# A two-block network on one core: which loads stand ahead of the first gathered rows, and where the last output product and two weight splits are put

## The chip, the cores and the metric

One core of a Trainium2 chip runs one program. The metric is the device time of an execution in microseconds (us); lower is better. Engines: TensorE (PE, its weight loads PEld), VectorE (DVE), ScalarE (ACT), GpSimd (POOL) and SyncE (SP). SP computes nothing: it issues most DMA transfers, one after the other, and each waits in this order for what it needs.

## The reference

Two transformer-like blocks over 512 tokens of 1024 features, in float32. The first has attention, a recurrent scan and a feed-forward net; the second has a convolution, attention, a cross attention and a mixture of experts. Only the end of the second matters here:

```python
x = x + cross_attention(rmsnorm(x, norm_xa_g[l]), rmsnorm(mem, norm_mem_g[l]), ...)   # o @ wo
x = x + hierarchical_moe(rmsnorm(x, norm_moe_g[l]), ...)
return rmsnorm(x, norm_final_g)

def hierarchical_moe(h, wg, bg, we, be, w_gate, w_up, w_down):
    ...            # router: best of 4 groups, best 2 of its 4 experts, their weights -> combine
    a = jnp.einsum("nd,edf->nef", hf, w_gate)
    b = jnp.einsum("nd,edf->nef", hf, w_up)
    u = jax.nn.silu(a) * b * combine[..., None]
    y = jnp.einsum("nef,efd->nd", u, w_down)
```

There are 16 experts with 256 inner features; each token goes to two.

## The kernel before

All float32 products are made from a high and a low part: `wsplit` (L350) writes a weight tile's high part with ACT (L354) and its low part with DVE (L357), and each k-step of `mm_as` (L375) is three matmuls (L380, L381, L382). The order of instructions on each engine is fixed when the program is built, by a list scheduler that goes by data, by buffers and by the order in which the code was written; `issue_after` keeps an instruction behind another one on its engine.

**Cross attention.** Tokens are four tiles of 128 (t = 0 to 3). `cross_out(t)` multiplies a tile by the output weights in two halves of 512 columns (n = 0, 1; 12 matmuls each) and DVE adds each half to the residual `x` (L1421). `route_unit(t)` then squares the row on ACT (L1463), transposes `x` on PE (L1467, tile `tp`), copies it (`xT`, L1470 and L1472), multiplies by the router's weights (L1481), finds group and experts on DVE (L1483 to L1511), and stores the normalised rows `hr` to DRAM (`rows_d`, L1503). When all four tiles are done, `slot_ids` (L1553) has the list of tokens of each expert, 96 at most.

**Experts.** The generator `expert(i)` (L1657) gathers its rows from `rows_d` with an indirect DMA that POOL issues (L1668, tile `gat`), transposes them (L1675), splits them (`eh`) and the four weight tiles `wl` (`ws`), multiplies 24 times, applies silu and product (`eu`), splits half of its down weights (`wed` to `wdh`, `wdl`; L1698), multiplies (the second half of the columns in plain float32, L1721) and adds its rows to DRAM. Seventeen experts run in a pipe (the 17th is a spare for an overfull expert).

**Loads.** An expert's weights are four transfers of 512 KB (`wl<-w_gu`, L347, into 20 buffers shared with other tiles) and four of 256 KB (`wed<-w_ed`, L1646): 3 MiB. The generator `fetch_all` lists them: the up weights of experts 0, 1 and 2, then by turns the down weights of expert i and the up weights of expert i + 3. PF2 of its steps are taken during the cross attention, NF = 4 (L1740) at each turn of the expert loop:

```python
for n, _ in enumerate(both()):
    if n >= PF0 and (n - PF0) % PF1 == 0 and n < PF0 + PF2 * PF1:
        next(self.fetches)
```

One step is one up transfer, or the four down transfers of an expert. PF2 = 18 steps are experts 0 to 3's up weights and experts 0 and 1's down weights; expert 4's up weights come at the first turn of the loop.

Of the kernel before, what the change touches and what calls it, by code (L numbers as in the profile page):

```python
# [14 lines left out]
AF = mybir.ActivationFunctionType  # L15
ALU = mybir.AluOpType
# [6 lines left out]
NT = 4  # L23
# [9 lines left out]
FD, NF = 2, 4  # L33
# [21 lines left out]
CAP = 96  # L55
NX = 2 * S // CAP
HEADS = (slice(0, 64), slice(64, 128))
LAG = (1, 1, 1, 1)
PF0, PF1, PF2 = 2, 1, 18


def f32(ap):
# [3 lines left out]
def fl(t):  # L66
    return t.rearrange("p a b -> p (a b)")
# [111 lines left out]
def run(gen):  # L179
    for _ in gen:  # L180
        pass


def chain(*gens):
    for g in gens:
        yield from g


def pipe(gens, width, newest=False):

    act, gens = [], iter(gens)
    while True:
        if len(act) < width:
            g = next(gens, None)
            if g is not None:
                act.append(g)
        if not act:
            return
        for g in act[::-1] if newest else list(act):
            if next(g, g) is g:  # L200
                act.remove(g)
        yield


def take(gen, n):
    for _ in range(n):
        if next(gen, gen) is gen:
            return
        yield
# [15 lines left out]
class Block:  # L225
# [18 lines left out]
    def open(self, ctx):  # L244
        self.xp = self.sb(ctx, "xp")
        self.wk = self.sb(ctx, "work")
        self.n = N1
        self.nsplit, self.stage = -1, 0
        nc, ins = self.nc, self.ins
        self.x = [self.xt("x") for _ in range(NT)]  # L250
        self.load_x(0, 2)
        nc.sync.dma_start(self.ident, ins["ident"])
        nc.sync.dma_start(self.vec, ins["vec"])
        self.w_lora = [self.load(ins["w_lora"][:, g:g + 2, :], 160) for g in range(0, KD, 2)]
        self.load_x(2, 4)
# [88 lines left out]

    def load(self, src, n=512, tag="r"):
        t = self.pt("wl", F32, tag)[:, :src.shape[1], :n]
        self.nc.sync.dma_start(t, src)  # L347
        return t

    def wsplit(self, t, tags="hl"):  # L350

        nc = self.nc
        hi, lo = (self.pt("ws", F32R, g)[:, :t.shape[1], :t.shape[2]] for g in tags)
        nc.scalar.activation(hi, t, AF.Copy)  # L354
        self.nsplit += 1
        eng = nc.gpsimd if self.nsplit % 4 in SP[self.stage] else nc.vector
        eng.tensor_tensor(lo, t, f32(hi), ALU.subtract)  # L357
        return [(hi[:, j], lo[:, j]) for j in range(t.shape[1])]
# [16 lines left out]
    def mm_as(self, ps, ws, act, t, m=128):  # L375
        nt = self.nc.tensor
        sl = slice(t * m, (t + 1) * m)
        for k, (wh, wl) in enumerate(ws):
            ah, al = act[k]
            nt.matmul(ps, ah[:, sl], wh, start=k == 0, stop=False)  # L380
            nt.matmul(ps, ah[:, sl], wl, start=False, stop=False)  # L381
            nt.matmul(ps, al[:, sl], wh, start=False, stop=k == len(ws) - 1)  # L382

    def proj(self, src, act, use, rest=None, ws=None):

# [1027 lines left out]
    def cross_out(self, t, wo, z):  # L1413
        yield
        yield
        a = [(z[:, 0, h * 128:(h + 1) * 128], z[:, 1, h * 128:(h + 1) * 128]) for h in range(4)]
        for n in range(2):
            ps = self.ps("mm")
            self.mm_as(ps, wo[n], a, 0)
            x = self.x[t][:, n]  # L1420
            self.nc.vector.tensor_tensor(x, x, ps, ALU.add)  # L1421
        yield


# [215 lines left out]
    def fetch_down(self, i):  # L1640

        w = []
        for ed in self.ed[i]:
            for k in range(2):
                w.append(self.ut("wed"))
                self.nc.sync.dma_start(w[-1], ed[:, k])  # L1646
        self.ed[i] = w
        yield

# [7 lines left out]
    def expert(self, i, add=True, skip=dict(bounds_check=S - 1, oob_is_err=False)):  # L1657

        nc = self.nc

        def lag(n):
            for _ in range(LAG[n]):
                yield

        raw = self.ew.pop(i)
        g = fl(self.xt("gat"))[:CAP]

        nc.gpsimd.indirect_dma_start(out=g, out_offset=None, in_=self.rows, **skip,  # L1668
                                     in_offset=bass.IndirectOffsetOnAxis(ap=self.ids[:CAP, i:i + 1], axis=0))
        yield from lag(3)  # L1670
        a = []
        for q in range(2):
            ps = self.ps("tp")[:, :4 * CAP]
            for k in range(4):
                nc.tensor.transpose(ps[:, k * CAP:(k + 1) * CAP], g[:, (4 * q + k) * 128:(4 * q + k + 1) * 128],  # L1675
                                    self.ident[:CAP, :CAP])
            z = self.pt("eh", F32R)
            h, l = (z[:, n, :4 * CAP] for n in range(2))
            self.split_to(h, l, ps)
            a += [(h[:, k * CAP:(k + 1) * CAP], l[:, k * CAP:(k + 1) * CAP]) for k in range(4)]  # L1680
        self.stage = 6
        with ExitStack() as c:

            for ins in self.last_of if i < 2 else ():
                c.enter_context(self.tc.issue_after(ins.ins))
            wg = [w for t in raw for w in self.wsplit(t)]
        yield from lag(0)
        ps = self.ps("mm")[:CAP]
        self.mm_as(ps, wg, a, 0, CAP)
        u = self.at("eu")[:CAP, :256]  # L1690
        nc.scalar.activation(u, ps[:, :256], AF.Silu)
        nc.vector.scalar_tensor_tensor(u, u, self.ws[:CAP, i:i + 1], ps[:, 256:], ALU.mult, ALU.mult)
        yield from lag(1)

        ed = self.ed.pop(i)
        hi, lo = self.pt("wdh", F32R, "r"), self.pt("wdl", F32R, "r")
        for k in range(2):
            self.split_to(hi[:, k], lo[:, k], ed[k])  # L1698
        wd = [(hi[:, k], lo[:, k]) for k in range(2)]
        tp = self.ps("tp")  # L1700
        for k in range(2):
            nc.tensor.transpose(tp[:, k * CAP:(k + 1) * CAP], u[:, k * 128:(k + 1) * 128], self.ident[:CAP, :CAP])
        z, zf = self.tg("euT", "a", F32R), self.at("euF")
        self.split_to(z[:, :2 * CAP], z[:, 256:256 + 2 * CAP], tp[:, :2 * CAP])
        nc.scalar.copy(zf[:, :2 * CAP], tp[:, :2 * CAP])
        a = [(z[:, k * CAP:(k + 1) * CAP], z[:, 256 + k * CAP:256 + (k + 1) * CAP]) for k in range(2)]
        yield from lag(2)
        if add:
            y = self.kt("ey")[:CAP]
        else:  # L1710
            oh = self.tg("oh", "u", F32R)[:CAP]
            self.onehot(oh, i)
            yh, yl = (self.pt("yl", F32R)[:CAP] for _ in range(2))
            self.last += [(oh, yh), (oh, yl)]
        for n in range(2):
            ps = self.ps("mm")[:CAP]
            if n == 0:
                self.mm_as(ps, wd, a, 0, CAP)
            else:
                for k in range(2):  # L1720
                    nc.tensor.matmul(ps, zf[:, k * CAP:(k + 1) * CAP], ed[2 + k], start=k == 0, stop=k == 1)  # L1721
            if not add:
                self.split_to(yh[:, n], yl[:, n], ps)
            else:
                nc.scalar.copy(y[:, n], ps)
        if add:
            nc.gpsimd.indirect_dma_start(
                out=self.acc, out_offset=bass.IndirectOffsetOnAxis(ap=self.ids[:CAP, i:i + 1], axis=0),
                in_=fl(y), in_offset=None, compute_op=ALU.add)
        yield  # L1730

    def moe(self, out):
        with ExitStack() as c:
            self.psum(c, "moe", mm=4, tp=3, r=1)
            p = pipe((self.expert(i, i < LAST) for i in range(17)), 16)
            ps, self.last = self.ps("r"), []
            self.route_weights()
            more = chain(self.weigh(self.ws[:CAP, 0:16], ps[:CAP, 0:16], self.rk, self.asg, 16), self.route_more())
            for n, _ in enumerate(p):
                run(take(self.fetches, NF))  # L1740
                for _ in range(6 if n == 0 else 2):
                    next(more, None)
                if n == GB:
                    gb = self.bcast_row(3)
            xs = [self.xt("fx") for _ in range(NT)]
            hs = [self.pt("fh") for _ in range(NT)]
            self.final(out, gb, xs, hs, self.last)
# [100 lines left out]
```

## Time and profile before

| | |
|---|---|
| time, median of 3 runs | 1434.97 us (1433.1 to 1436.15) |
| the profiled execution | 1433.15 us, of which the span of instructions is 1431.3 us |
| busy share of the span | PE 95%, PEld 75%, DVE 61%, ACT 44%, POOL 4% |
| chain that ended last, by engine | PE 84%, DVE 9%, DMA 2%, ACT 2% |

The span lies 1.85 us below the execution's own time. A busy PE includes matmuls that wait in its pipeline. The cross attention ends near 1213 us, the routing near 1227, the experts run from 1236 to about 1411, and the final norm ends the span at 1431.3.

### The profile page before, as it was taken

The page shows a single profiled execution, that of the slowest core. Times are in us where ns is not written, and L with a number is a line of the kernel's source. Part 1 is how long each engine was busy: PE and PEld are TensorE (multiplying, and loading weights), DVE is VectorE, ACT ScalarE, POOL GpSimd, SP SyncE. Part 2 cuts the span into 40 slices and gives each one's busy share as a digit, 9 for nine tenths or more (in the row PEclk, how much of TensorE's full clock was granted, in tenths as well). Part 3 has the DMA queues.
Part 4 walks back from the last instruction along what each step waited for, and adds up shares of the span by engine and source line. Part 5 has one row for each costly group of instructions (what it writes and reads, how often), then busy time and mean ns, then how long its engine had stood idle before and what let it go on. Part 6 is the DMA issues. An engine that isn't in the chain of part 4 may idle for free.

```text
span 1431.3 us, 21684 instructions
## 1 busy us (share of the span) xinstructions
PE 1364.3 (95%) x8366; PEld 1073.1 (75%) x8366; DVE 874.6 (61%) x2035; ACT 623.3 (44%) x1143; POOL 52.6 (4%) x45
## 2 busy tenths in 40 slices
PE   5999999999799999999999999999999999699996
PEld 5877777677588888888888887776788887466663
DVE  5247465664875235434467475996555566799875
ACT  5244335543344333322434414445432453477873
POOL 0000000000000000000000000000000000232211
PEclk9999999999999999999999999999999999699998
DMA  5222420021223223233143214222131535799984
GB/s 209 102 76 76 156 78 20 13 90 60 89 75 118 88 89 118 71 107 118 61 146 109 84 45 162 75 74 75 62 117 60 176 134 198 239 310 335 330 285 146
DMA packets 67759, 178.01 MB, mean 124 GB/s; under 512 B 17144, under 2 KB 18552, under 8 KB 67648
## 3 DMA queue, kind: packets, MB, share of 16 engines
q1 hardware_dynamic: 58676, 156.39, 32.7%
q0 software_dynamic: 3584, 10.10, 3.2%
q10 hardware_dynamic: 5388, 10.06, 2.0%
q8 instruction: 68, 1.11, 0.3%
q14 instruction: 43, 0.35, 0.1%
HBM read 163.12 MB, written 15.88 MB: 125 GB/s over the span
## 4 chain that ended last, share of the span: by engine, by line
PE 84%; DVE 9%; DMA 2%; ACT 2%; issue 2%; SPq 0%; DVEq 0%; ACTq 0%
PE mm L371 11%; PE mm L372 11%; PE mm L373 11%; PE mm L380 10%; PE mm L382 10%; PE mm L381 10%; PE q L967 3%; PE mm L1721 2%; DVE ws L357 2%; PE acc L537 2%; PE s L512 1%; PE tp L531 1%; DVE cacc L1113 1%; PE mm L918 1%; PE tp L918 1%
## 5 line engine op out<-in xcount | busy, mean ns | idle before, releaser
L357 DVE TENSOR_TENSOR ws<-wl,ws 128x1024 fp32r<-128x1024 f32 (+2 forms) x238 | 280.6, 1192 | 140.4 <-ACT ws L354 134.0
L354 ACT ACTIVATE ws<-wl 128x1024 fp32r<-128x1024 f32 (+2 forms) x238 | 244.2, 1033 | 182.4 <-PE mm L382 111.0
L371 PE MATMUL mm<-hT,ws 128*128 128x512 f32 (+3 forms) x872 | 314.5, 365 | 1.6 <-ACT qT L565 0.7
L372 PE MATMUL mm<-hT,ws 128*128 128x512 f32 (+3 forms) x872 | 314.1, 362 | 1.0 <-DVE hT L427 1.0
L373 PE MATMUL mm<-hT,ws 128*128 128x512 f32 (+3 forms) x872 | 312.6, 361 | 0.0
L371 PEld LDWEIGHTS mm<-hT,ws 128*128 128x128 f32 (+2 forms) x872 | 162.0, 187 | 30.6 <-ACT qT L565 1.4
L372 PEld LDWEIGHTS mm<-hT,ws 128*128 128x128 f32 (+2 forms) x872 | 163.0, 187 | 27.2 <-DVE hT L427 2.4
L373 PEld LDWEIGHTS mm<-hT,ws 128*128 128x128 f32 (+2 forms) x872 | 162.8, 187 | 24.9 <-DVE ws L357 0.2
L380 PE MATMUL mm<-ws,ff 128*128 128x512 f32 x256 | 100.0, 391 | 0.0
L382 PE MATMUL mm<-ws,ff 128*128 128x512 f32 x256 | 99.7, 389 | 0.0
L381 PE MATMUL mm<-ws,ff 128*128 128x512 f32 x256 | 99.6, 389 | 0.0
L1113 DVE SCALAR_TENSOR_TENSOR cacc<-sig,vec,cacc 128x507 f32<-128x507 f32 (+25 forms) x120 | 86.1, 732 | 1.6
L1068 DVE TENSOR_TENSOR ur<-ur 128x512 f32<-128x512 f32 x32 | 22.1, 692 | 82.3 <-ACT ff L1067 82.3
L380 PE MATMUL mm<-ws,eh 128*96 128x512 f32 x136 | 56.3, 414 | 1.6 <-ACT eh L423 1.6
L1064 ACT ACTIVATE ur<-mm 128x512 f32<-128x512 f32 x32 | 19.0, 594 | 87.1 <-PE mm L373 87.1
L382 PE MATMUL mm<-ws,eh 128*96 128x512 f32 x136 | 55.7, 410 | 0.7 <-DVE eh L424 0.6
L382 PEld LDWEIGHTS mm<-ws,ff 128*128 128x128 f32 x256 | 48.0, 188 | 10.0
L381 PEld LDWEIGHTS mm<-ws,ff 128*128 128x128 f32 x256 | 48.1, 188 | 9.9
L380 PEld LDWEIGHTS mm<-ws,ff 128*128 128x128 f32 x256 | 48.1, 188 | 9.9
L381 PE MATMUL mm<-ws,eh 128*96 128x512 f32 x136 | 55.0, 404 | 0.0
L521 ACT ACTIVATE sp<-sp,mx 128x128 f32<-128x128 f32 (+3 forms) x64 | 35.7, 558 | 29.8 <-DVE mx L519 29.1
L1087 DVE TENSOR_TENSOR f<-f,mm 128x512 f32<-128x512 f32 x24 | 16.5, 686 | 49.8 <-PE mm L382 49.8
(436 smaller groups left out, 2351.0 us busy)
## 6 DMA issues: line engine op xcount, KB each, us to landing
wl<-w_gu SPq DMA_DIRECT2D x68, 512.0 KB
wl<-w_p SPq DMA_DIRECT2D x60, 512.0 KB
wed<-w_ed SPq DMA_DIRECT2D x68, 256.0 KB
wl<-w_up SPq DMA_DIRECT2D x32, 512.0 KB
wl<-w_dn SPq DMA_DIRECT2D x32, 512.0 KB
wl<-w_out SPq DMA_DIRECT2D x16, 512.0 KB
x<-x SPq DMA_DIRECT2D x8, 512.0 KB
gram_d<-gb SPq DMA_DIRECT2D x8, 256.0 KB
```

The lines of the kernel that those rows point to most:

```text
L354: nc.scalar.activation(hi, t, AF.Copy)
L357: eng.tensor_tensor(lo, t, f32(hi), ALU.subtract)
L371: nt.matmul(ps, wh[:, c0:c0 + m], ah[:, sl], start=k == 0, stop=False)
L372: nt.matmul(ps, wh[:, c0:c0 + m], al[:, sl], start=False, stop=False)
L373: nt.matmul(ps, wl[:, c0:c0 + m], ah[:, sl], start=False, stop=k == len(ws) - 1)
L380: nt.matmul(ps, ah[:, sl], wh, start=k == 0, stop=False)
L381: nt.matmul(ps, ah[:, sl], wl, start=False, stop=False)
L382: nt.matmul(ps, al[:, sl], wh, start=False, stop=k == len(ws) - 1)
L521: nc.scalar.activation(sps[h][:, :n], sps[h][:, :n], AF.Exp, scale=-1.0, bias=mxs[h][:, 0:1], accum_out=ls[h])
L537: nc.tensor.matmul(out_ps[64 * h:64 * h + 64, i * 128:(i + 1) * 128], vs[h](j), pts[h][:, j * 128:(j + 1) * 128], start=j == 0, stop=j == i)
L967: nc.tensor.matmul(ps[a], lhs[a], rhs[a], start=n == 0, stop=n == len(terms) - 1)
L1113: nc.vector.scalar_tensor_tensor(acc[:, d:], up[:, 0:S - d], w(30 - d), acc[:, d:], ALU.mult, ALU.add)
```

## The change

```diff
-PF0, PF1, PF2 = 2, 1, 18
+PF0, PF1, PF2 = 2, 1, 13
...
     def load(self, src, n=512, tag="r"):
         t = self.pt("wl", F32, tag)[:, :src.shape[1], :n]
-        self.nc.sync.dma_start(t, src)
+        self.hold(self.nc.sync.dma_start(t, src))
         return t
+
+    def hold(self, dma):
+
+        if self.behind is not None:
+            self.tc.add_manual_dep(dma.ins, self.behind.ins.name, ...)
...
             self.nc.vector.tensor_tensor(x, x, ps, ALU.add)
+            if n == 0 and t == NT - 1:
+                yield
...
-        nc.gpsimd.indirect_dma_start(out=g, out_offset=None, in_=self.rows, **skip,
+        ga = nc.gpsimd.indirect_dma_start(out=g, out_offset=None, in_=self.rows, **skip,
...
+        if i == 0:
+            self.behind = ga
...
+            wg = [w for t in raw[:2] for w in self.wsplit(t)] if i == 0 else []
             for ins in self.last_of if i < 2 else ():
                 c.enter_context(self.tc.issue_after(ins.ins))
-            wg = [w for t in raw for w in self.wsplit(t)]
+            wg += [w for t in raw[len(wg) // 2:] for w in self.wsplit(t)]
...
-        for k in range(2):
-            self.split_to(hi[:, k], lo[:, k], ed[k])
+        with ExitStack() as c:
+
+            if i < 2:
+                c.enter_context(self.tc.issue_after(act.ins))
+                c.enter_context(self.tc.issue_after(mul.ins))
+            for k in range(2):
+                self.split_to(hi[:, k], lo[:, k], ed[k])
...
             for n, _ in enumerate(p):
-                run(take(self.fetches, NF))
-                for _ in range(6 if n == 0 else 2):
+                run(take(self.fetches, NF + (5 if n == 0 else 0)))
+                self.behind = None
+                for _ in range(2 if n > 1 else 0):
                     next(more, None)
```

In the cross attention only 13 steps of loads are taken: the up weights of experts 0 to 2 and the down weights of expert 0. The other five, with expert 4's four, come at the first turn of the expert loop, and each of these is made to wait for the first gather to have landed (`hold`). `cross_out(3)` hands on between its halves. Two weight tiles of expert 0 may be split before the routing's end, and the splits of experts 0's and 1's down weights stand behind their silu and product. The weighing (`weigh`, L1543) is written behind the first expert's product, the planning of the spare (`route_more`) starts two turns later, and the second expert's transposes stand behind that product.

On SP, where the loads of the last stage begin, before (`wl<-w_gu` is an up transfer, `wed<-w_ed` a down transfer, `rows_d<-hr` the store of a token tile's rows):

```order
L347 DMA wl<-w_gu 128x1024 x12
L1503 DMA rows_d<-hr 128x1024
L347 DMA wl<-w_gu 128x1024
L1646 DMA wed<-w_ed 128x512 x4
L347 DMA wl<-w_gu 128x1024 x3
L1503 DMA rows_d<-hr 128x1024
L1646 DMA wed<-w_ed 128x512 x4
L1503 DMA rows_d<-hr 128x1024
L347 DMA wl<-w_gu 128x1024
L1503 DMA rows_d<-hr 128x1024
L347 DMA wl<-w_gu 128x1024 x3
L1646 DMA wed<-w_ed 128x512 x4
```

and in the change, from the third of the four row stores on, with the semaphores that each one waits for (`DMASW0` is that of POOL's gather):

```order
L1513 DMA rows_d<-hr 128x1024 [waits DMAHW6_49,DVE_49]
L1513 DMA rows_d<-hr 128x1024 [waits DMAHW0_49,DVE_49]
L347 DMA wl<-w_gu 128x1024 [waits DMASW0_49,DMAHW1_49,PE_49,Activation_49]
L347 DMA wl<-w_gu 128x1024 [waits DMAHW4_49,DMAHW2_49]
L347 DMA wl<-w_gu 128x1024 [waits DMAHW3_49,PE_49]
L347 DMA wl<-w_gu 128x1024 [waits PE_49,Activation_49]
L1656 DMA wed<-w_ed 128x512 [waits DMAHW5_49]
L1656 DMA wed<-w_ed 128x512 [waits DMAHW6_49]
L1656 DMA wed<-w_ed 128x512 [waits DMAHW7_49]
L1656 DMA wed<-w_ed 128x512 [waits DMAHW0_49]
L347 DMA wl<-w_gu 128x1024 [waits DMAHW1_49,Activation_49]
```

Before, eight up transfers and four down transfers stand between the first row store and the last up transfer that comes ahead of expert 2's down weights. In the change these twelve stand behind the last row store, and the first of them waits for the gather; all that follow on SP wait with it.

On PE at the end of the cross attention, before (`x_3451` is `x` of t = 2, `x_4201` that of t = 3; `mm_11021` is the second half of t = 3's output product):

```order
L380 MATMUL mm_11021<-ws_10291,oX_10792 128x512
L381 MATMUL mm_11021<-ws_10292,oX_10792 128x512
L382 MATMUL mm_11021<-ws_10291,oX_10792 128x512
L1467 MATMUL tp_11039<-ident_64,x_3451 128x128 x4
L1467 MATMUL tp_11045<-ident_64,x_3451 128x128 x4
L1481 MATMUL mm_11067<-cst_65,xT_11035 128x24 x4
L1467 MATMUL tp_11098<-ident_64,x_4201 128x128 x4
L1481 MATMUL mm_11067<-cst_65,xT_11035 128x24 x4
```

and in the change (`mm_10991` and `mm_11037` are the two halves of t = 3):

```order
L388 MATMUL mm_10991<-ws_10280,oX_10790 128x512
L389 MATMUL mm_10991<-ws_10279,oX_10790 128x512
L1477 MATMUL tp_11009<-ident_64,x_3451 128x128 x4
L1477 MATMUL tp_11015<-ident_64,x_3451 128x128 x4
L387 MATMUL mm_11037<-ws_10285,oX_10790 128x512
L388 MATMUL mm_11037<-ws_10286,oX_10790 128x512
L389 MATMUL mm_11037<-ws_10285,oX_10790 128x512
```

The eight transposes of t = 2 move from behind the second half to between the halves.

On DVE in the same place, before (`hr` is of t = 2; the `x` rows are the two adds of t = 3, and the first is not shown here):

```order
L325 SCALAR_TENSOR_TENSOR nr_q<-nr_q 128x1
L326 SCALAR_TENSOR_TENSOR nr_o<-nr_q,nr_o 128x1
L1421 TENSOR_TENSOR x<-x,mm 128x512
L1502 SCALAR_TENSOR_TENSOR hr<-x,nr_o,gbc 128x1024
L1472 COPY xT<-tp 128x512
L1483 SCALAR_TENSOR_TENSOR cst<-mm,nr_o,cst 128x24
L1485 MAX cst<-cst 128x8
L1472 COPY xT<-tp 128x512
```

and in the change:

```order
L326 SCALAR_TENSOR_TENSOR nr_o<-nr_q,nr_o 128x1
L1482 COPY xT<-tp 128x512
L1512 SCALAR_TENSOR_TENSOR hr<-x,nr_o,gbc 128x1024
L364 TENSOR_TENSOR ws<-wl,ws 128x1024
L1429 TENSOR_TENSOR x<-x,mm 128x512
L1493 SCALAR_TENSOR_TENSOR cst<-mm,nr_o,cst 128x24
L1495 MAX cst<-cst 128x8
L1496 MAX_INDEX gi<-cst 128x8
L1498 TENSOR_TENSOR og<-cst,gi 128x4
L1482 COPY xT<-tp 128x512
```

The low part of one of expert 0's weight tiles (`ws<-wl,ws`) now stands ahead of the last add to `x`, and the copy `xT` of t = 2 ahead of `hr`.

## Rows read from the trace of the kernel before

**Rows 1.** Busy time by stretch: busy us of each engine, granted clock, DMA share, GB/s

```profile
1230.00:1240.00 10.00, 3.13 (x16) 1.95 (x15) 5.52 (x12) 2.29 (x4) 6.84 (x4) 0.50 1.01 313
1240.00:1250.00 10.00, 9.30 (x39) 6.55 (x40) 5.94 (x13) 5.33 (x8) 0.96 (x1) 0.78 0.72 200
1250.00:1260.00 10.00, 9.95 (x47) 6.31 (x46) 10.00 (x61) 7.78 (x15) 1.46 (x2) 1.00 0.97 306
1260.00:1384.00 124.00, 124.00 (x590) 82.24 (x588) 106.58 (x191) 98.03 (x161) 32.61 (x23) 1.00 1.03 328
```

**Rows 2.** Moved by the DMA engines, 1230 to 1384.3 us, by queue

```profile
GB/s 356 309 237 178 218 284 303 300 335 298 284 295 336 325 304 368 322 356 321 314 343 366 311 315 300 366 349 354 318 316 348 297 356 310 316 347 265 371 406 316
DMA packets 18274, 49.04 MB, mean 318 GB/s; under 512 B 2745, under 2 KB 2745, under 8 KB 18261
q1 hardware_dynamic: 14901, 39.57, 73.3%
q0 software_dynamic: 3360, 9.31, 26.5%
```

**Rows 3.** The chain that ended last, 1350 us on: start, us, what

```profile
1374.49 9.69 DMA wl<-w_gu
...
1388.24 0.43 PE mm L382
...
1391.23 0.24 PE mm L380
```

**Rows 4.** Timeline of ACT at the end of the expert stage

```profile
1384.26 1.06 ACT L354 ACTIVATE ws<-wl 128x1024 fp32r<-128x1024 f32 x1 [3.62 <-DMA wl<-w_gu]
1385.23 0.85 ACT L423 ACTIVATE eh<-tp 128x384 fp32r<-128x384 f32 x2
```

**Rows 5.** Timeline of SP, the queue that issues the loads

```profile
1134.46 33.50 SPq L347 DMA_DIRECT2D wl<-w_gu  x12
...
1184.87 0.97 SPq L347 DMA_DIRECT2D wl<-w_gu  x1
...
1187.87 5.92 SPq L347 DMA_DIRECT2D wl<-w_gu  x3
...
1202.86 2.25 SPq L1646 DMA_DIRECT2D wed<-w_ed  x4
...
1219.22 0.33 SPq L347 DMA_DIRECT2D wl<-w_gu  x1
...
1223.95 2.90 SPq L347 DMA_DIRECT2D wl<-w_gu  x3
1227.19 1.98 SPq L1646 DMA_DIRECT2D wed<-w_ed  x4
```

**Rows 6.** Timeline, first gather to the first expert's transposes

```profile
1228.13 1.25 POOL L1668 DMA_INDIRECT gat<-rows_d,cst  x1 [458.49 <-DMA wl<-w_gu]
...
1236.27 1.54 PE L1675 MATMUL tp<-ident,gat 96*128 96x96 f32 x8 [5.22 <-DMA gat<-rows_d,cst]
```

**Rows 7.** The gathered tile over the whole run, last line of its view

```profile
DMA to landing us min/median/max: 6.0/7.6/11.0
```

**Rows 8.** Timeline of the routing of the last two token tiles

```profile
1213.20 0.69 DVE L1421 TENSOR_TENSOR x<-x,mm 128x512 f32<-128x512 f32 x1 [1.52 <-PE mm L382]
...
1220.55 0.15 DVE L331 TENSOR_SCALAR ms<-ssq 128x1 f32<-128x1 f32 x1
...
1227.00 0.16 DVE L1553 SCALAR_TENSOR_TENSOR cst<-r,ide 96x16 int32<-96x16 f32 x1
```

**Rows 9.** Timeline, split of the second expert's down weights in the cross stage

```profile
1206.66 1.30 ACT L423 ACTIVATE wdh<-wed 128x512 fp32r<-128x512 f32 x2 [4.44 <-DMA wed<-w_ed]
```

**Rows 10.** What SP waited for, 1180 to 1400 us: total, times, longest

```profile
SPq L347 <- DMA wl<-w_gu: 31.3, 23, 2.7
SPq L1646 <- DMA wed<-w_ed: 21.8, 28, 2.5
SPq L1646 <- PE mm L1721: 14.5, 5, 4.8
```

More of the change, by code (lines that the diff above doesn't have):

```diff
@@ L247, in open @@
         self.n = N1
-        self.nsplit, self.stage = -1, 0
+        self.nsplit, self.stage, self.behind = -1, 0, None
         nc, ins = self.nc, self.ins
@@ L346, in load @@
         t = self.pt("wl", F32, tag)[:, :src.shape[1], :n]
-        self.nc.sync.dma_start(t, src)
+        self.hold(self.nc.sync.dma_start(t, src))
         return t
+    def hold(self, dma):
+        if self.behind is not None:
+            self.tc.add_manual_dep(dma.ins, self.behind.ins.name,
+                                   mybir.DependencyInfo(mybir.DependencyClass.Sync, mybir.DependencyReason.DATA),
+                                   reason="hold")
     def wsplit(self, t, tags="hl"):
@@ L381, in mm_as @@
             nt.matmul(ps, ah[:, sl], wl, start=False, stop=False)
-            nt.matmul(ps, al[:, sl], wh, start=False, stop=k == len(ws) - 1)
+            o = nt.matmul(ps, al[:, sl], wh, start=False, stop=k == len(ws) - 1)
+        return o
     def proj(self, src, act, use, rest=None, ws=None):
@@ L1645, in fetch_down @@
                 w.append(self.ut("wed"))
-                self.nc.sync.dma_start(w[-1], ed[:, k])
+                self.hold(self.nc.sync.dma_start(w[-1], ed[:, k]))
         self.ed[i] = w
@@ L1673, in expert @@
             ps = self.ps("tp")[:, :4 * CAP]
-            for k in range(4):
-                nc.tensor.transpose(ps[:, k * CAP:(k + 1) * CAP], g[:, (4 * q + k) * 128:(4 * q + k + 1) * 128],
-                                    self.ident[:CAP, :CAP])
+            with ExitStack() as c:
+                if i == 1:
+                    c.enter_context(self.tc.issue_after(self.last_of[2].ins))
+                for k in range(4):
+                    nc.tensor.transpose(ps[:, k * CAP:(k + 1) * CAP], g[:, (4 * q + k) * 128:(4 * q + k + 1) * 128],
+                                        self.ident[:CAP, :CAP])
             z = self.pt("eh", F32R)
@@ L1682, in expert @@
         with ExitStack() as c:
+            wg = [w for t in raw[:2] for w in self.wsplit(t)] if i == 0 else []
             for ins in self.last_of if i < 2 else ():
                 c.enter_context(self.tc.issue_after(ins.ins))
-            wg = [w for t in raw for w in self.wsplit(t)]
+            wg += [w for t in raw[len(wg) // 2:] for w in self.wsplit(t)]
         yield from lag(0)
         ps = self.ps("mm")[:CAP]
-        self.mm_as(ps, wg, a, 0, CAP)
+        last = self.mm_as(ps, wg, a, 0, CAP)
+        if i == 0:
+            self.last_of.append(last)
+            run(self.weights)
         u = self.at("eu")[:CAP, :256]
-        nc.scalar.activation(u, ps[:, :256], AF.Silu)
-        nc.vector.scalar_tensor_tensor(u, u, self.ws[:CAP, i:i + 1], ps[:, 256:], ALU.mult, ALU.mult)
+        act = nc.scalar.activation(u, ps[:, :256], AF.Silu)
+        mul = nc.vector.scalar_tensor_tensor(u, u, self.ws[:CAP, i:i + 1], ps[:, 256:], ALU.mult, ALU.mult)
         yield from lag(1)
@@ L1696, in expert @@
         hi, lo = self.pt("wdh", F32R, "r"), self.pt("wdl", F32R, "r")
-        for k in range(2):
-            self.split_to(hi[:, k], lo[:, k], ed[k])
+        with ExitStack() as c:
+            if i < 2:
[3 more added lines that the diff above has]
+                self.split_to(hi[:, k], lo[:, k], ed[k])
         wd = [(hi[:, k], lo[:, k]) for k in range(2)]
@@ L1737, in moe @@
             self.route_weights()
-            more = chain(self.weigh(self.ws[:CAP, 0:16], ps[:CAP, 0:16], self.rk, self.asg, 16), self.route_more())
+            self.weights = self.weigh(self.ws[:CAP, 0:16], ps[:CAP, 0:16], self.rk, self.asg, 16)
+            more = self.route_more()
             for n, _ in enumerate(p):
-                run(take(self.fetches, NF))
-                for _ in range(6 if n == 0 else 2):
+                run(take(self.fetches, NF + (5 if n == 0 else 0)))
+                self.behind = None
+                for _ in range(2 if n > 1 else 0):
                     next(more, None)
```

## The prediction

> **What bounds the kernel now.** The page's chain is 84% PE, an average over a program with several stages; the change touches only the last, so I read that stage. First the stretches [rows 1]: from 1260 to 1384 us PE is busy for all 124 us, which looks like PE's bound. But the same row has the 16 DMA engines at a share of 1.03 and 328 GB/s. Both are full, and a full PE row cannot say which of the two waits, since waiting matmuls count as busy. The view by queue [rows 2] has no slice below 265 GB/s from 1250 on; over all of it went 49.04 MB in 154.3 us, 73.3% of the time for SP's loads (39.57 MB) and 26.5% for POOL's gathers and sums (9.31 MB). The chain of waits decides [rows 3]: near the end it leaves PE and goes through an up-weight load, issued at 1374.49 and taking 9.69 us. ACT stands idle 3.62 us for it and splits it at 1384.26 [rows 4]; behind that split, in ACT's fixed order, stands the split of gathered rows `eh` (1385.23) that PE needs next. SP's own waits agree [rows 10]: 31.3 and 21.8 us for earlier loads to land, against 14.5 for a matmul to free a buffer. So the experts are fed ahead at first, the lead shrinks, and at the last expert it is gone. What ends the kernel is the landing of the last expert's first load, 47.0 us before the span's end; that lands when all bytes ahead of it have moved.
>
> Ahead of the stage it is different: after the routing PE waits for the first gather. POOL issued it at 1228.13 and PE transposed its rows at 1236.27, after 5.22 us of idling [rows 6], with the clock at 0.50 of full, its 1.2 GHz level [rows 1].
>
> **The change, part by part.**
>
> *Loads.* Before, experts 3 and 4's up weights and expert 1's down weights were issued between 1184.87 and 1226.85, beside the cross attention and the routing [rows 5]; all but the tail of the last one was through by 1230. That is 8 x 512 KB and 4 x 256 KB, 5.24 MB. After the change all of it waits for the gather, and everything behind it on SP (the weights of experts 2 and 5 to 16) waits too. SP computes nothing, so only ACT's splits and PE behind them can feel it. What is the price of 5.24 MB in a full stage? SP's queue took 73.3% of 154.3 us, 113.1 us, for 39.57 MB [rows 2]: 2.86 us a MB, **+15.0 us**. The best slice (406 GB/s) gives 12.9, the stretch 1240 to 1250 (200 GB/s [rows 1]) 26.2; I take the mean of the stage, whose kind of traffic it is.
>
> *When the loads start.* The gather's issue moves by the routing (below) from 1228.13 to about 1227.1. From issue to landing the 17 gathers took 6.0 to 11.0 us, median 7.6 [rows 7]; the first took 8.1. With no load in flight I take the low end, 6.0: landed at 1233.1. Less cannot be excluded; the floor is one issue (1.25 us [rows 6]) and 0.39 MB (96 rows of 4 KB) at 328 GB/s, 1.2 us. For the first held bytes to flow I add 1.5: no row has an idle queue's first byte, the bounds are SP's 0.33 us for an issue [rows 5] and about 3 us (1202.86 to the split at 1206.66, less 0.75 us for 256 KB at 350 GB/s [rows 5, 9]). So 1234.6 instead of 1230, **+4.6**. The gather's own 0.39 MB lies ahead of that point now, **-1.2**.
>
> The Trainium skill speaks against the hold (DMA: Bandwidth & Descriptors, section Queues, rings and completion order): each DMA engine takes the queues with work by turns, packet by packet, so a gather is not behind all that SP has queued. By that it would lose no more than its own 1.2 us to the loads, and land at 1234.0 instead of 1233.1, 0.9 us more in the sum. The 6.0 us in the full stage [rows 7] fit that better than a queue behind megabytes.
>
> *What the stage can give back.* Between 1230 and 1260 the DMA engines moved 313, 200 and 306 GB/s against 328 later [rows 1]: 1.65 MB less than they could. Here the 20 buffers were full of weights loaded ahead: rows 10 have SP waiting for matmuls (longest 4.8 us). With buffers empty at the gather this hole closes: **-5.0** (0 if it was something else).
>
> *Routing.* The eight transposes of t = 2 move ahead of the second half of t = 3's product, so DVE has t = 2's copy and logits earlier. In the trace the last add to `x` is at 1213.20, t = 2's choices run on DVE up to t = 3's norm at 1220.55, and the list of tokens is at 1227.00 [rows 8]. About half a us of t = 2's work leaves DVE's row behind t = 3's copy, and expert 0's and 1's down splits no longer stand in it; against it one low split of 1.2 us stands ahead of the last add. I take 1 us gained, bounds 3 gained and 1.2 lost; it is in the 4.6.
>
> *Down splits, early up splits, weighing.* Costed at nothing. Two down splits and the 4.44 us for which ACT waited for expert 1's load [rows 9] leave the cross attention, where PE has its own matmuls in front; after the change they lie beside the second expert's 24 up matmuls. Without that cover they cost 2 x 1.3 us, once. Expert 1's down weights come behind expert 3's 2 MiB: 3.15 MB at 2.86 from 1234.6, about 1244, and one round trip. By then PE has two experts' up products and one down product in front; a stall there moves no byte and so not the end.
>
> *Sum.* 15.0 + 4.6 - 1.2 - 5.0 = **+13.4 us**, on the profiled execution's 1433.15: 1446.6. On the median, 1434.97, it would be 1448.4; I give **1447**. With halves of the bounds taken together the case's own range is 1440 to 1455.
>
> **The rivals.**
>
> *PE's bound, faster.* If the last wait of 3.62 us were an accident and the DMA engines had room, the held bytes would be absorbed and the start would count: PE begins 1236.27 - 1233.1 = 3.2 us earlier, and up to 3.6 of the wait goes. 1426 to 1430, say 1429. It decides from the point where the last expert's load lands before PE wants it. For it: the early experts have a lead of tens of us (expert 4's weights are issued by 1226.85 and its turn comes four experts later). Against it: the chain ends in a load, and the two queues' shares sum to 99.8% [rows 2]. A page of the Trainium skill gives this rival its argument: Perfetto Trace Analysis, section Identifying the Most-Contended Engine, holds that the share of busy DMA engines misleads and moved bytes should be read, and HBM Reference, section Specifications (TRN2), has about 425 GB/s for one core alone; by that figure (an estimate) 5.24 MB cost 12.3 us and the stage would have a quarter of its capacity unused. No slice of rows 2 is above 406 GB/s, and gathers of single rows share them. Chance 0.12.
>
> *Absorbed, no change.* SP's waits for buffers are starved loads, not just full ones: if all of the 14.5 us [rows 10] and not 5.0 come back, the sum is +3.9; with a gather 3 us sooner it is 1434. For it: rows 10. Against: the share of 1.03 beside those waits. 1432 to 1438, chance 0.08.
>
> *Slower still.* When the lead is gone each of the last experts waits, not only one, and PE's clock follows: after the wait at the end a matmul still takes 0.43 us at 1388.24 and 0.24 only at 1391.23 [rows 3]; the first is the lower level's pace. Some 4 us at half the pace lose 2. Three more such dips, where PE then comes later than the loads, bring 6 us: 1450 to 1458. Chance 0.12.
>
> The hold itself is certain to act: the order lists the gather's semaphore on the first held load.
>
> **How the numbers follow.** Forecast 0.68, the three rivals 0.12, 0.08, 0.12. A change below 0.2% (2.9 us) can't be told from none here. Slower: 0.68 + 0.12 = 0.80; same 0.08 (part of its cases slower, as many faster); faster 0.12. The range reaches down to the edge of the absorbed case and up through most of the slower one: 1436 to 1456, which leaves out the faster rival and a few of either end.
>
> **What would show it.** Right: SP idle from the last row store to about 1233; the first transposes some 3 us earlier; the DMA engines full from 1235 to about 1397 without the hole at 1240; ACT waiting for up weights at several of the last experts, the chain going through loads, and the last expert's first split 12 to 14 us later than 1384.26. Wrong: that split before 1388, or no waits for loads; then the stage was PE's. If the gather lands as late as before, the contention was not its delay.

## The result, and the profile after

The changed kernel takes 1445.26 us, median of 4 runs (1443.47 to 1449.17), against 1434.69 us for the kernel before (4 runs, 1433.10 to 1436.15): a ratio of 1.0069, 95% interval 1.0053 to 1.0086, or **10.6 us slower**. The forecast was 1447, slower.

The profiled execution after is the slowest of the four (1449.17 us, span 1447.4), and part of that has nothing to do with the change: it is late before the changed code begins. In the timeline of SP, the first twelve loads of experts' weights, at 1134.46 us in [rows 5], begin 5.95 us later:

```profile
1140.41 33.10 SPq L347 DMA_DIRECT2D wl<-w_gu  x12
...
1205.51 22.95 SPq L1513 DMA_DIRECT2D rows_d<-hr  x3
1238.34 1.97 SPq L347 DMA_DIRECT2D wl<-w_gu  x4
```

So 5.95 is taken off every time of after that is set beside one of before. The spans then differ by 1447.4 - 1431.3 - 5.95 = 10.15 us, close to the 10.6 us between the medians. The third row is the hold: after the last row stores SP issues nothing until 1238.34 (1232.39 when corrected).

The timelines of POOL and PE answer to [rows 6]:

```profile
1232.69 2.11 POOL L1678 DMA_INDIRECT gat<-rows_d,cst  x1 [458.67 <-DVE cst L1580]
...
1238.25 1.54 PE L1690 MATMUL tp<-ident,gat 96*128 96x96 f32 x8 [7.00 <-DMA gat<-rows_d,cst]
```

Corrected, the gather is issued at 1226.74 instead of 1228.13 and its rows are transposed at 1232.30 instead of 1236.27: 5.56 us after its issue instead of 8.14. That part of the change works: PE begins the experts 4.0 us sooner.

What it gives for that is in the stretches, counted from the first transposes (columns as in [rows 1]: PE, PEld, DVE, ACT, POOL busy, clock, DMA share, GB/s):

```profile
1238.25:1248.25 10.00, 9.46 (x43) 6.80 (x43) 5.45 (x10) 5.50 (x9) 2.20 (x3) 0.78 0.97 279
1248.25:1258.25 10.00, 7.60 (x45) 5.48 (x46) 9.81 (x23) 6.03 (x7) 0.67 (x1) 1.00 1.03 347
1258.25:1268.25 10.00, 9.78 (x40) 5.83 (x38) 9.38 (x53) 7.55 (x15) 2.48 (x2) 0.83 1.04 375
1268.25:1399.79 131.54, 123.43 (x580) 80.35 (x578) 103.03 (x195) 93.84 (x160) 31.35 (x22) 1.00 1.03 333
```

PE was busy for all 124 us of the long stretch of [rows 1]; now it is idle for 8.1 of 131.5. The DMA engines are busy from the start, without the hole that the kernel before has at 1240 us. By queue, from the first held load to the last expert's first split (1238.3 to 1399.8 us):

```profile
DMA packets 19824, 53.76 MB, mean 333 GB/s; under 512 B 2885, under 2 KB 2885, under 8 KB 19809
...
q1 hardware_dynamic: 16602, 44.74, 77.7%
q0 software_dynamic: 3207, 8.85, 24.4%
```

Against [rows 2] SP's queue has 5.17 MB more to bring behind the gather: the 5.24 MB of the forecast, but for what was under way at the edges. What waits for it shows in ACT's waits from 1230 us (total, times, longest) and in its timeline:

```profile
ACT wdh L431 <- DMA wed<-w_ed: 18.3, 11, 4.2
...
ACT ws L361 <- DMA wl<-w_gu: 6.2, 7, 3.7
```

The same view of the kernel before, from 1230 us, has nearly as much waiting for up weights and next to none for down weights:

```profile
ACT ws L354 <- DMA wl<-w_gu: 4.7, 4, 3.6
ACT wdh L423 <- DMA wed<-w_ed: 0.3, 1, 0.3
```

The timeline of ACT after:

```profile
1276.30 0.63 ACT L431 ACTIVATE wdh<-wed 128x512 fp32r<-128x512 f32 x1 [4.19 <-DMA wed<-w_ed]
...
1297.19 0.63 ACT L431 ACTIVATE wdh<-wed 128x512 fp32r<-128x512 f32 x1 [2.68 <-DMA wed<-w_ed]
...
1399.79 1.06 ACT L361 ACTIVATE ws<-wl 128x1024 fp32r<-128x1024 f32 x1 [3.73 <-DMA wl<-w_gu]
```

The last row answers to [rows 4]: 1393.84 corrected, against 1384.26, 9.6 us later. The first two rows are not at the end of the stage but near its start, and they wait for down weights. The chain that ended last says the same; it now runs through loads (start, us, what):

```profile
1284.65 12.52 DMA wed<-w_ed
1297.25 12.92 DMA wed<-w_ed
...
1336.53 10.12 DMA wed<-w_ed
1346.67 12.82 DMA wl<-w_gu
1359.56 10.46 DMA wed<-w_ed
...
1389.66 10.05 DMA wl<-w_gu
```

### The profile page after: what moved, and what is told of

Read it like the earlier page. It is cut to its first block, busy times and chain, and to the rows that moved or that the text cites. A ratio compares the mean times of both kernels' runs of the same rounds, so it can differ in the third digit from the quotient of the medians.

```text
span 1447.4 us, 21689 instructions
## 1 busy us (share of the span) xinstructions
PE 1371.1 (95%) x8366; PEld 1078.5 (75%) x8366; DVE 876.1 (61%) x2035; ACT 622.1 (43%) x1143; POOL 50.7 (4%) x45
## 4 chain that ended last, share of the span: by engine, by line
PE 78%; DVE 9%; DMA 9%; ACT 2%; issue 2%; SPq 0%; ACTq 0%; DVEq 0%; POOLq 0%
PE mm L378 11%; PE mm L379 11%; PE mm L380 11%; PE mm L387 9%; PE mm L389 9%; PE mm L388 9%; DMA wed<-w_ed 5%; PE q L975 3%; DVE ws L364 2%; PE acc L545 2%; DMA wl<-w_gu 2%; PE s L520 1%; PE tp L539 1%; DVE cacc L1121 1%; PE tp L926 1%
```

## The experiments

Theory 1 is the prediction's: the loads that the change holds back set the end, since the stage is full of transfers. Theory 2: another edit costs the time. Theory 3: the late start does, not the number of bytes. Theory 4: the place behind the cross attention does, held or not. Theory 5, formed after the first four runs: the loss is made by the first experts, which stand without weights, and PE is the bound afterwards. Each run is given as its ratio to the kernel before on the same chip, with 95% interval; us are that ratio's difference from 1, times 1435. By this the change is at +9.9 us, by the medians at +10.6. Where times of two profiles are set beside each other, each is less its offset: the start of its first expert load less 1134.46, as above.

**1. The load edit alone.** The kernel before with this part:

```
-PF0, PF1, PF2 = 2, 1, 18
+PF0, PF1, PF2 = 2, 1, 13
...
-        self.nc.sync.dma_start(t, src)
+        self.hold(self.nc.sync.dma_start(t, src))
...
+        if i == 0:
+            self.behind = ga
...
-                run(take(self.fetches, NF))
+                run(take(self.fetches, NF + (5 if n == 0 else 0)))
```

> The kernel before with the load edit alone (12 loads, 5.24 MB, not issued before the routing, and the loads behind the first gather held for its rows); product, down splits, early splits and weighing as before. Theory 1, the held bytes set the end because the stage is full of transfers: the whole loss is here, +9 to +13 us, 1444 to 1448 (a little over the full change, since the gather is not issued 1.4 us sooner). Theory 2, the loss comes from the other edits (the weighing and the down splits put among the first experts): no change, 1433 to 1437. In the trace under theory 1: the last expert's first split about 10 us later than in the kernel before.

Measured: 1.0087 [1.0066, 1.0107], +12.5 us, as theory 1 said. But the trace does not show theory 1's way. Timelines of ACT, DVE and PE:

```profile
1255.66 1.30 ACT L430 ACTIVATE wdh<-wed 128x512 fp32r<-128x512 f32 x2 [15.65 <-DMA wed<-w_ed]
...
1256.32 0.69 DVE L431 TENSOR_TENSOR wdl<-wed,wdh 128x512 fp32r<-128x512 f32 x1 [10.62 <-ACT wdh L430]
1256.93 0.16 DVE L1553 COPY cst<-r 96x16 f32<-96x16 f32 x1
...
1257.14 0.26 PE L1570 MATMUL r<-cst,c 128*128 128x16 bf16 x4 [9.72 <-DVE cst L1553]
```

ACT stands 15.65 us at the second expert's down split, whose load is held; DVE's half of that split stands 10.62 us, the copy that PE needs is behind it in DVE's order, and PE stands 9.72 us. From 1280 on no engine waits over half a us for a load. So here the order of the splits made the loss and PE carried it to the end. In the full change these splits stand behind the first experts' silu and product, and this stall is absent. The run is slower for another reason than the change is; alone it decides nothing.

**2. Everything but the load edit.** The changed kernel with PF2 = 18, no extra loads at the first turn (n = 0), and no hold:

```
-        if i == 0:
-            self.behind = ga
```

> The changed kernel without its load edit: 18 steps of loads ahead of the routing as before, nothing held; the other three edits stay. Theory 1 (held bytes): 1432 to 1436, at or a little under the kernel before, since what is left is a routing some 1 us earlier and hidden splits. Theory 2 (the other edits cost the time): 1443 to 1446. The first gather should take about 8 us again, as its rows share the engines with expert 4's weights.

Measured: 1.0008 [0.9997, 1.0019], +1.1 us. In sum the other edits are worth nothing that can be told; one by one they were not run. As the cause of the whole loss theory 2 falls; a part of it comes back below. The gather again took 9.2 us to its transposes (1232.70 to 1241.92).

**3 and 4. Fewer bytes held; nothing held.** Run 3 has PF2 = 18 and keeps the hold, which then catches 2.1 MB. Run 4 is the change without the two lines above.

> The changed kernel with 18 steps of loads ahead of the routing, so that the hold catches only expert 4's four up loads, 2.1 MB, instead of 5.24 MB. Theory 1, price by bytes: 3.15 MB less at 2.86 us a MB is 9.0 us less, of which the hole that the empty buffers filled takes some back: 1436 to 1441. Theory 3, the late start alone costs the time and not the number of bytes: as the changed kernel, 1443 to 1447. Rival, bytes that lie beside a PE-bound stage cost nothing until the lead is used up: no change to before, 1433 to 1436.

> The changed kernel with the hold taken away: 13 steps of loads ahead of the routing, the other 5.24 MB behind the first gather in the program but free to start when the last row store has been issued, some 12 us earlier than when held. Theory 1: the queue's bytes start 12 us sooner, so nearly all of the loss goes, 1433 to 1438; the gather then lands 7 to 9 us after its issue instead of 5.5. Theory 4, that the bytes are lost by being behind the cross attention, hold or no hold: 1441 to 1445.

Measured: 1.0003 [0.9989, 1.0018] and 1.0003 [0.9991, 1.0014]. Both take the whole loss away. Run 4 is the plainest of all: it differs from the change only in the hold. The same 5.24 MB stand behind the cross attention, most of them some 11 us earlier (from 1221.6 against 1232.4 on SP), and theory 4 falls. So the hold on these 5.24 MB is what costs the 10 us. Run 3 says that a hold that catches 2.1 MB costs nothing in sum; theory 3 falls, and theory 1's price by bytes, which had 1436 to 1441, is at its edge or under it: 1436.0, on a chip where the kernel before takes 1436.4. The gather went from issue to transposes in 5.3 us in run 3 (held) and 9.6 in run 4 (not held).

**5 to 8. Bytes taken out of the stage, late or early.** The second half of the down weights is not loaded for some experts, and their second product uses the first half again; the matmuls stay.

```
+        few = i >= 8
-        for ed in self.ed[i]:
+        for ed in self.ed[i][:1] if few else self.ed[i]:
...
-        self.ed[i] = w
+        self.ed[i] = 2 * w if few else w
```

Run 5 is the changed kernel with this, run 6 the kernel before, run 7 experiment 1; run 8 is the changed kernel with `i < 9` in its place.

> The changed kernel, with the second half of the down weights not loaded for experts 8 to 16 (their second product uses the first half again, so the output is not the reference's): 9 x 0.52 MB, 4.7 MB less for the DMA engines, all of it behind the first experts, with the same matmuls. Theory 1 (the landing of the last loads sets the end): at 2.86 to 3.1 us a MB 13 to 15 us less, down to where PE sets the end: 1431 to 1436. Theory 5 (the loss is made by the first experts, which stand without weights between 1250 and 1320, 8.4 us of PE idle, and PE is the bound afterwards): only the waits after 1340 and at the last expert go, 3 to 6 us, 1439 to 1443.

> The kernel before with the same 4.7 MB not loaded (the output is not the reference's): the floor that PE sets when no late load is waited for. Theory 1 in its strict form (before too is set by bytes): 1425 or less. If before is balanced, with PE no more than the 3.6 us of the last wait behind: 1431 to 1434. Theory 5: 1431 to 1435.

> The load edit alone, in which ACT stood 15.7 us before the down split of expert 1 and no load was waited for at the end, with the same 4.7 MB not loaded (the output is not the reference's). If its loss is that stall in ACT's and DVE's fixed order and not the bytes: no change, 1446 to 1449. If bytes: 1435 to 1438.

> The changed kernel with the second half of the down weights not loaded for experts 0 to 8 (the output is not the reference's): of the held loads 8 x 0.52 = 4.2 MB less, now at the start of the stage. Theory 1: bytes ahead of the last load count alike wherever they lie, so the time is that of the run with fewer late bytes within 2 us. Theory 5: here nearly all of the loss goes (1432 to 1437) and in the run with fewer late bytes it does not.

Measured: run 5 1.0018 [1.0000, 1.0036], run 6 0.9972 [0.9955, 0.9989], run 7 1.0077 [1.0048, 1.0106], run 8 0.9990 [0.9972, 1.0007]. Run 7 hardly moves from experiment 1's 1.0087: there the loss is the stall and not the bytes. In the change bytes count: 4.7 MB fewer at the end (run 5) take 0.51%, 7.3 us. That is half of the 13 to 15 us of theory 1, and the run lies between the ranges of theories 1 and 5. With 4.2 MB fewer at the start (run 8) 0.79% goes, 11.3 us, but not by bytes alone: the scheduler built this run in another order, with the weighing elsewhere (see the edits costed at nothing), so that early bytes are worth more than late ones, theory 5's share, is not shown. Run 6 is the floor that PE sets in the kernel before, 4.0 us under it; run 5, with the same late bytes gone, stays 6.6 us above it. The stretch 1300 to 1320 us of run 5 and then of run 6 shows where:

```profile
1300.00:1320.00 20.00, 16.86 (x72) 10.36 (x71) 12.97 (x32) 10.60 (x20) 4.14 (x3) 0.91 1.00 326
```

```profile
1300.00:1320.00 20.00, 20.00 (x102) 13.53 (x101) 18.93 (x38) 15.67 (x27) 5.00 (x4) 1.00 1.04 337
```

PE loses 3.1 us there and, in the stretches from 1260 to 1300, 3.0 more; ACT's waits for down weights in run 5 are three, at 1271, 1291 and 1305 us (4.2, 2.6 and 5.1 us). Of the 13.9 us by which the change lies above PE's floor (9.9 + 4.0), 7.3 go with late bytes, and 6.6 stay. These 6.6 are not all made by loads: run 4, in which ACT waits for no load over 0.4 us, already lies 4.4 us above run 6. Run 5 lies 2.2 us above run 4; its 6.1 us of PE's idle time, less the 3.5 us by which it begins the experts sooner (first transposes at 1231.86 against 1235.37, each less its offset), are of that size.

**9 to 11. The dose.** The changed kernel with PF2 = 16 (3.67 MB held), PF2 = 20 with the hold (1.05 MB), and PF2 = 22, where nothing is left to hold and expert 4's loads are issued between the stores of rows.

> The changed kernel with 16 steps of loads ahead of the routing: the hold catches one up load of expert 3, the four of expert 1's down weights and the four of expert 4's up weights, 3.67 MB. Between no loss for 2.1 MB held and +10.6 us for 5.24 MB, a straight price of 3.4 us a MB gives +5.3 us, 1439 to 1442. If the loss is made by one transfer that comes late (expert 1's down weights, held here and in the change, not with 2.1 MB): +9 to +11, 1444 to 1447. If it is made by expert 3's up weights as a whole: within 2 us of no loss.

> The same with 20 steps: two of expert 4's up loads early, two (1.05 MB) held for the first gathered rows. Theory 1: 1.05 MB less behind the gather than with 2.1 MB held, up to 3 us less, 1432 to 1435; if that kernel was already at PE's bound, no change, 1434 to 1437.

> The changed kernel with 22 steps of loads ahead of the routing: expert 4's four up loads now stand ahead of the last two stores of rows in SP's order, some 20 us sooner than in the kernel before, where the DMA engines have room (share 0.30 from 1190 to 1230 us); nothing is held. If the last loads set a part of the time of the kernel before too, the 4.0 us by which fewer late bytes made it faster are to be had: 1431 to 1434. If SP stands at these loads for buffers, the row stores behind them are late and the routing with them: over 1438. Otherwise as before.

Measured, with runs 3 and 4 and the change:

| held, MB | ratio, 95% | us | first transposes, less the offset | from there to the end |
|---|---|---|---|---|
| none (run 4) | 1.0003 [0.9991, 1.0014] | +0.4 | 1235.37 | 197.2 |
| 1.05 (run 11) | 0.9988 [0.9973, 1.0002] | -1.7 | 1233.11 | 199.1 |
| 2.10 (run 3) | 1.0003 [0.9989, 1.0018] | +0.4 | 1232.17 | 201.1 |
| 3.67 (run 9) | 1.0030 [1.0017, 1.0044] | +4.3 | 1232.09 | 203.3 |
| 5.24 (the change) | 1.0069 [1.0053, 1.0086] | +9.9 | 1232.30 | 209.2 |
| none, 22 steps early (run 10) | 1.0036 [1.0020, 1.0051] | +5.2 | 1237.42 | 197.0 |

The times bend: nothing that can be told for the first 2 MB, then some 3 us a MB. That the last step (3.6 us a MB) is steeper than the one before it (2.5) lies within the intervals. The two columns on the right, one profile each, say what the flat start is made of. A hold brings the first transposes 2.3 to 3.3 us sooner than in run 4, and all that follows takes longer from the first MB held on: at 2.10 MB it is 3.9 us longer, against a start 3.2 us sooner. So the first 2 MB are not free; the sooner gather pays for them. The two parts are rough, since runs 3 and 11 were built in another order of the weighing; runs 4 and 9 and the change share one order there and give +0.4, +4.3 and +9.9 us.

Expert 1's down weights, held at 3.67 MB too, do not make the change's loss by themselves. The last line lost for a reason of its own, in the routing. SP, ACT and DVE of run 10, then DVE of run 3:

```profile
1209.40 5.73 SPq L347 DMA_DIRECT2D wl<-w_gu  x3
1220.69 8.78 SPq L1513 DMA_DIRECT2D rows_d<-hr  x2
```

```profile
1223.40 0.58 ACT L1480 COPY xT<-tp 128x512 f32<-128x512 f32 x1 [4.15 <-DMA rows_d<-hr]
```

```profile
1216.41 0.69 DVE L1482 COPY xT<-tp 128x512 f32<-128x512 f32 x1 [1.64 <-PE mm L389]
...
1219.38 1.28 DVE L1512 SCALAR_TENSOR_TENSOR hr<-x,nr_o,gbc 128x1024 f32<-128x1024 f32 x1
```

```profile
1212.34 0.69 DVE L1482 COPY xT<-tp 128x512 f32<-128x512 f32 x1
...
1212.95 1.27 DVE L1512 SCALAR_TENSOR_TENSOR hr<-x,nr_o,gbc 128x1024 f32<-128x1024 f32 x1
```

Three loads wait on SP for buffers, but they do not keep the row stores back: the last of them is issued by 1215.13, and the third store goes out at 1220.69, when DVE has just made its rows. These rows are late, 5.1 us against run 3 when each time is less its offset, since the copy `xT` of t = 2 is made only behind a matmul of the product, 2.8 us late, and the rows stand behind it and behind the logits in DVE's order. The loads and `xT` share the 20 buffers, so early loads could have taken the one that `xT` needed; that is not shown. ACT then waits 4.15 us for a tile that the late store must release, and the gather is issued 4.0 us later than in run 3. No expert waited over 0.4 us for a weight, and from the first transposes to the end the run takes 197.0 us, as runs 2 (197.1) and 4 (197.2) do. So with the loads early the start of the experts sets the end; it is 2.05 us later than in run 4, of the 4.7 us between their times, and the rest is open. The best of all, 1.05 MB held, cannot be told from the kernel before.

**12. The change with few bytes.** As run 8, for all 17 experts (8.9 MB less).

> The changed kernel with the second half of the down weights not loaded for any expert (the output is not the reference's): PE's bound of the changed kernel, with few waits for loads. If its sooner first gather is worth 3 us where bytes don't count: 1428 to 1431, 2 to 3 us under the kernel before with fewer late bytes (1431). If not, 1431 to 1433, like the run with fewer early bytes. Theory 5 in part (the first experts still wait for held loads at half the down weights): 1433 to 1436.

Measured: 0.9993 [0.9979, 1.0007], no sooner than before and, with more bytes taken out, not under run 6's 0.9972. ACT still waited three times for down weights, 7.3 us in all, so this is not PE's bound. The 4.0 us by which PE starts sooner did not reach the end in any run here; what took them is in the columns above and in the edits costed at nothing.

## Why the prediction was right

**What bounds the kernel.** Right for the changed kernel: the chain goes through loads to the last expert's first one, letting them start sooner brings all of the time back (run 4), and taking late bytes out brings part of it (run 5). For the kernel before it was too strong. Run 6 has PE's floor only 4.0 us lower, about the one wait of 3.62 us in [rows 4]: loads and PE are nearly balanced there.

**The sum.** On the profiled executions the forecast's +13.4 us at the last expert's split came out as +9.6 us, under the 12 to 14 that it named as its sign, and the tail behind it added 0.6. By its terms, of which the third is what the other two leave:

| term | forecast | measured | how |
|---|---|---|---|
| bytes behind the gather, its own 0.39 MB taken off | +13.8 | +14.8 | 53.76 - 49.04 = 4.72 MB at before's 318 GB/s |
| start of the held loads | +4.6 | +2.4 | 1238.34 - 5.95 - 1230 |
| the hole given back | -5.0 | -7.6 | 53.76 MB at 318 GB/s are 169.1 us, and took 161.5 |

The bytes were sized well. The start was too late by three guesses: the gather was issued 0.4 us sooner than assumed, its rows were used 5.56 us after that and not 6.0, and the 1.5 us that I added for an idle queue's first bytes is in the measured rate and not in the start. The hole was the largest miss. The first 30 us moved 279, 347 and 375 GB/s, 10.0 MB, against 8.2 MB in [rows 1], worth 5.5 us; the other 2, nearly, are a stage that ran at 333 instead of 329 GB/s in its remainder, which no step had. Bytes came out 1.0 us above their term, start and hole together 4.8 us below theirs. The forecast's single price per MB, good for the whole, hides the bend that the dose shows.

**The gather.** Right, and by more than forecast. From issue to transposes it took 5.0 to 5.6 us where the loads behind it were held (the change and the eight other runs with a hold), and 6.6 to 9.6 where they were not (before, runs 2, 4, 6 and 10), so the contention was its delay. The Trainium skill (DMA: Bandwidth & Descriptors, section Queues, rings and completion order) has the engines take the queues by turns, packet by packet; by the prediction's estimate from it the first gather would lose 1.2 us to the loads. These rows do not agree with that size: without the hold and nothing else changed it takes 4.1 us more (9.6 in run 4 against 5.56), and in the kernel before 2.6 more (8.14).

**Where the waits are.** Half right. ACT waits for up weights at the last experts, as forecast, but hardly longer than in the kernel before (6.2 us against 4.7); what the change adds are waits for down weights (18.3 us against 0.3), from 1276 us on. The order on SP puts an expert's four down loads behind the next experts' up loads, so with a short lead they are the first to be late. "A stall there moves no byte and so not the end" holds only while the loads set the end; run 5, with the late bytes gone, still lost 6.1 us of PE's time where three such stalls lie.

**The edits costed at nothing.** In sum right against the kernel before (run 2), but run 2 still waits 2.81 us for the last expert's first load, as the kernel before does 3.62, and such a wait hides what PE does ahead of it. Where no load is waited for, the edits cost time: run 4 lies 4.4 us above run 6, and from the first transposes to the end it takes 197.2 us against run 6's 190.2 (195.0 in the kernel before, its wait included). These 7 us stand against the 4.0 by which the experts start sooner. In the kernel before the weighing ran while PE waited for the gather:

```profile
1227.36 2.87 PE L1543 MATMUL r<-ohw 128*96 128x16 f32 x16 [0.72 <-DVE ohw L1542]
```

In the change its sixteen matmuls stand by twos among the second expert's products, and PE stands there for DVE (timeline of PE after):

```profile
1256.10 0.34 PE L1553 MATMUL r<-ohw 128*96 128x16 f32 x2 [1.09 <-DVE ohw L1552]
1257.39 0.25 PE L1573 MATMUL r<-cst,c 128*128 128x16 bf16 x4 [0.95 <-DVE cst L1556]
```

In the second 10 us from the first transposes PE is busy 7.60 us, against 9.95 in the kernel before, and 7.60 in run 2 too, where the DMA share is 0.55 and no load is short (before, then run 2):

```profile
1246.27:1256.27 10.00, 9.95 (x52) 6.80 (x51) 9.46 (x63) 7.79 (x15) 1.29 (x2) 1.00 0.94 288
```

```profile
1251.92:1261.92 10.00, 7.60 (x48) 5.48 (x48) 9.81 (x24) 5.90 (x8) 0.45 (x1) 1.00 0.55 185
```

After that idling the granted clock of the next 10 us is 0.83: part of them at 1.2 GHz. Both together are some 4 of the 7 us (an estimate: 2.4 us idle, and 1.7 lost in 3.4 us at half the pace); the rest is open. Runs 8 and 12, with the same edits, are busy for 9.85 us there, since the scheduler built them in another order. Run 8 has fourteen of the sixteen in one piece behind the first expert's product:

```profile
1240.37 1.28 PE L1553 MATMUL r<-ohw 128*96 128x16 f32 x14
```

Run 12 has the same; run 3 has them ahead of the first expert's product and idles in the first 10 us instead (busy 6.69 us), and run 11 lies between. So a run whose edit lies elsewhere can still move the weighing.

The cover that I named for the down splits is real, as experiment 1 shows without it: not the 2 x 1.3 us of the splits but 9.72 us of PE's time. That price was wrong, since I counted the splits' own time and not what stands behind a split whose load is late.

**The rivals.** PE's bound, faster: no run with the sooner start came clearly faster, not even with 8.9 MB taken out (run 12), though ACT still waited there. Absorbed: up to 2.1 MB held the time is that of the kernel before, since the sooner gather pays for it (table of the dose). Slower still: the granted clock is 1.00 from 1268 to the last expert's split, so the dips did not come. The argument from busy DMA engines held for this stage, though the share alone says little: at 1.03 to 1.04 the rows of after move from 333 to 375 GB/s, which is the caution of the Trainium skill (Perfetto Trace Analysis, section Identifying the Most-Contended Engine).

## What to carry to other kernels

Where transfers and TensorE are balanced, price a hold on loads by two numbers: what the transfer that it favours gains, and how much longer the stage behind it gets. Here 2 MB held cancelled the gain, and from there on each MB cost some 3 us: find that edge by holding back a little more each time, not by one price per byte. A part that is slower alone can be so for another reason than the whole: the load edit alone lost 12.5 us to a split in ACT's fixed order, the full change 10.6 us to held loads, and only taking the hold away and taking bytes out told them apart. Work that fills a wait is not free to move: the weighing cost nothing while PE waited for the gather, and PE idled for it among the experts. And where a scheduler fixes the order, compare the orders of two runs before a difference is put down to the edit.

## What the runs showed of the hardware

Executions of one kernel spread over some 10 us, and in these profiles most of the spread comes from ahead of the changed stage: the first expert load starts anywhere from 1131.16 us (run 12) to 1141.54 (run 4), and what is left of the span from there (296.8 us before, 307.0 after, 298.8 in run 3) follows the timed ratios within 2.6 us in all 12 runs. Between the profiles of before and after 4.4 of the 5.95 us are there by 433 us, where the stretch 200 to 400 us shows a granted clock of 0.98 and 0.95; why it differs is not shown.
